# Hybrid attention and convolution layer: far scores over full rows, one head in a bank, parameters transposed later, and a new instruction order

## The chip, the core and the metric

The kernel runs on one core of a Trainium2 chip. The metric is the time of one execution in microseconds (us), taken on the device. PE is TensorE, the matrix engine; DVE is VectorE, ACT is ScalarE, POOL is GpSimd, and SP is the engine that issues most DMAs.

## The reference, cut to what matters

One layer works on x of 1024 tokens by 1024 columns, in fp32. A normed x is projected into seven parts; an attention branch and a convolution branch use them, and one output projection joins both.

```python
h = rmsnorm(x, norm_g)
q, k, v, a_gate, c_val, c_glu, c_gate = split(h @ w_in)   # 1024, 256, 256, 1024, 1024, 1024, 1024 columns
...
for window, dilation in ((128, 1), (512, 4), (2048, 16)):  # 16 query heads, 4 key heads, 64 wide
    o, lse = dilated_window_attention(q, k, v, slopes, window, dilation)
...
y_att = sum(softmax(lses) * outs) * silu(a_gate)
c = layernorm(causal_conv31(c_val * sigmoid(c_glu)) + conv_b) * ln_g + ln_b
y_conv = silu(c) * silu(c_gate)
x = x + concat([y_att, y_conv]) @ w_out
return rmsnorm(x, final_norm_g)
```

## The kernel before, in words

Every fp32 value that TensorE multiplies is split into a high and a low part (names ending in h or hi, l or lo), and a product is the sum of two or three matmuls over these parts. The 5632 columns of the input projection are made 128 at a time: the function `inproj` loads a 128-column block of weights (`raw`), casts it to `wh` and gets `wl` by a DMA that POOL issues, and fills a PSUM bank `ps` with 48 matmuls of 512 columns for the block. What reads a finished bank (`use`) is named in the place that asks for the projection: `project_q` writes the scaled queries of two heads to `qs`, with the high part in the 64 rows of the head's own half and the low part in the other 64 rows (DVE, line 269), and ACT casts them to `qf`, which holds the same queries with the four tokens of a stride apart.

Attention goes by pairs of heads, 0 to 7 (`attend`). Its scores are of two kinds. Near scores, `sc_near`, are those within 128 tokens; far scores, `sc_far`, serve the dilations 4 and 16. A call of `score` makes the scores of both heads for a few units, one PSUM bank `sc` for each head. There are two such banks. `kdh` holds the high part of the keys in both halves of its rows, `kdl` the low part. A near unit is two matmuls over all 128 rows: queries by `kdh` (which is high by high and low by high in one), and queries by `kdl`. The call far0 has 4 units of 96 columns for each head, far1 and far3 have 2 units of 224, and the near calls have 2 units of 256 (one of the first call's is 128). DVE adds a table and takes a minimum from each unit in PSUM (line 284), and ACT takes the exponent; then the bank is free for the next call. The sums over values go to `comb`, which is stored to a tile `y` by SP for one half and added into it by a DMA of POOL (`add_into`, line 298) for the other; then DVE multiplies `y` by the gate `ag` (line 269, 128x1024).

For far scores before the change, the matmuls by `kdl` use only the 64 rows of the head's own half (so low queries by low keys are left out); the two heads' matmuls alternate, one in the upper and one in the lower half of the array, and all of a call form one operation of the plan:

```python
second[j].append((to, q[r], keys(kl)[r], False, last))
...
pl.mm(first + [c for both in zip(*second) for c in both])
```

The convolution is 31 taps on DVE (`convolve`, buffers `c` and `t`, line 269). `parameters` loads the taps, `conv_b`, `ln_g` and `ln_b` as rows and transposes them on PE into the bank `par_ps`.

The order of the work is not written by hand. A class `Plan` records every operation with a modelled cost, and its `order` schedules the list for all engines: a priority from the program position, less a boost of `TUNE`; limits of how many buffers of a group are alive (`LIMITS`); and which projections stand beside which head pair and convolution block (`SECTIONS`). The result is one fixed order for each engine, which the engine follows on the chip and in which it waits where something is late. All matmuls carry line 237 and all transposes line 235.

Of the kernel before, what the change touches and what calls it, by code (L numbers as in the profile page):

```python
# [16 lines left out]
P = 128  # L17
# [6 lines left out]
DH = 64  # L24
# [8 lines left out]


LIMITS = {"x": 5, "raw": 1, "raw_oc": 1, "raw_oa": 2, "wh": 4, "wl": 3, "tab": 1, "e": 7, "pt": 4, "vs": 4, "vc":
          4, "turn": 2, "opsa": 2, "score": 2, "hc": 7, "c": 7, "t": 1, "g": 1, "gl": 7, "y": 2, "ag": 4, "cc": 5,
          "qs": 6, "qf": 4, "kdh": 9, "kdl": 5, "yc": 1, "ya": 2, "zc": 8, "za": 3}

RESERVE = {"e": 7, "pt": 3}
BANKS = {"mm": 3, "sc": 2, "tp": 2, "o": 1}  # L40
WARM = 26
LATE = C_CG + 6 * P
MORE = (8, 8)
TUNE = {"w": 225, "use": 120, "ln": 75, "att": 240, "conv": 15, "wo": 165, "woa": -350, "ap": 50, "wait": 0.2116}
SECTIONS = [("k0 q0 h1 v", 0), ("h2 a0 q1", 1), ("h3 a1 q2", 1), ("a2 q3 h4", 1), ("h5 k1 a3 q4", 1), ("h6 a4 q5",
            1), ("c0 h7 a5 q6", 1), ("a6 c1 a7 q7 c2", 1), ("c5 c4 c3", 1), ("c6 c7", 0)]


def score_tables():
# [112 lines left out]
class Plan:  # L162
    LATENCY = 0.2
    ahead = 267
    near = 574
# [138 lines left out]
    def order(self):  # L304
# [55 lines left out]
        while len(out) < n:  # L360
            best = None
            for e, todo in ready.items():
                now, pick = None, None
                for i in sorted(todo, key=self.prio.__getitem__):
                    t = start_of(i)
                    if t is None:
                        continue
                    soon = t - TUNE["wait"] if self.prio[i] < i - 300 else t
                    if now is None or soon < now - 1e-9:
# [94 lines left out]
def layer_kernel(tc, x, norm_g, w_in, conv_w, conv_b, ln_g, ln_b, w_out, fin_g, tab, out):  # L464
# [3 lines left out]
    def pool(name, space=None):  # L468
# [4 lines left out]
    pl = Plan(tc, {  # L473
        "big": (sb, "big", 4), "c8": (sb, "c8", 1), "c4": (sb, "c4", 33), "c2": (sb, "c2", 5), "st": (sb, "st", 16),
        "sx": (sb, "sx", 6),
        **{k: (ps, k, BANKS[k]) for k in PSUM_KINDS},
    }, LIMITS)
# [35 lines left out]
    def c4(shape, name, dtype=F32):  # L513
        group = name.rstrip("0123456789_")
        return pl.buf("c4", shape, dtype, name, group=group if group in pl.limits else None)

    def bank(kind, name, group=None):
        return pl.buf(kind, [P, 512], F32, name, group=group)
# [24 lines left out]
    hhi = [pl.buf("big", [P, ND, 512], F32R, f"hhi{i}") for i in range(2)]  # L543
# [61 lines left out]
    def parameters():  # L605
        pl.load(rows[0:KT, :], conv_w)
        for j, v in enumerate((conv_b, ln_g, ln_b)):
            pl.load(rows[KT + j:KT + j + 1, :], v.rearrange("(o d) -> o d", o=1))
        b = bank("o", "par_ps")
        pl.mm([(b[:, c * NPAR:(c + 1) * NPAR], rows[0:NPAR, c * P:(c + 1) * P], ident[0:NPAR, 0:NPAR], None, None)  # L610
               for c in range(8)])
        pl.act(par, b[:, 0:8 * NPAR], AF.Copy)
        pl.ts(half_w, par, 0.5, None, ALU.mult)
        for p in range(8):
            g = half_w[:, p * NPAR:p * NPAR + KT + 1].split(2)
            t = taps[:, p * 48:p * 48 + 48].split(3)
            pl.act(t[:, :, 0], g[:, :, 0], AF.Copy)
            pl.act(t[:, 0:15, 1], g[:, 0:15, 1], AF.Copy)
            pl.act(t[:, 0:1, 2], g[:, 0:1, 0], AF.Copy)
            pl.tt(t[:, 1:16, 2], g[:, 1:16, 0], g[:, 0:15, 1], ALU.add)  # L620


    def load_raw(col):
        raw = c4([P, ND, P], f"raw{col}")
        pl.load(raw, w_in[:, col:col + P].rearrange("(c p) n -> p c n", p=P))
        return raw

    def split_w(col, raw, split=split_dma):
        wh, wl = c4([P, ND, P], f"wh{col}", F32R), c4([P, ND, P], f"wl{col}", F32R)
        split(wh, wl, raw)  # L630
        return wh, wl

    def load_w(col):
        if col in ready:
            return ready[col]
        old, pl.boost = pl.boost, TUNE["w"]
        w = split_w(col, load_raw(col), split_r if col >= LATE else split_dma)
# [3 lines left out]
    def inproj(col, use, cuts=((0, 512), (0, 512))):  # L641
        wh, wl = load_w(col)
        for half in range(2):
            b = bank("mm", f"ps{col}_{half}")
            for n0, n1 in zip(cuts[half], cuts[half][1:]):
# [5 lines left out]
                for c in range(0, ND, 2):  # L651
                    pl.mm([(b[:, n0:n1], wl[:, c + i, :], hhi[half][:, c + i, n0:n1], False, c + i == ND - 1)
                           for i in range(2)])
            pl.boost = TUNE["use"]
            use(half, b, slice(half * 512, half * 512 + 512))
# [46 lines left out]
    qs, qf = {}, {}  # L702
# [20 lines left out]
    ag = {}  # L723
# [15 lines left out]
    hc = {}  # L739

    def project_h(p):
        hc[p] = c4([P, 2, 512], f"hc{p}")

        def use_glu(half, b, cs):
            pl.act(hc[p][:, :, half * 256:half * 256 + 256], b.parity(), AF.Tanh, scale=0.5)

        def use_val(half, b, cs):
            h = hc[p][:, :, half * 256:half * 256 + 256]
            pl.stt(h, h, 1.0, b.parity(), ALU.add, ALU.mult)
        cuts = ((0, 512), (0, 512)) if p else ((0, 256, 512), (0, 512))  # L750
        glu, val = inproj(C_GLU + p * P, use_glu, cuts), inproj(C_VAL + p * P, use_val, cuts)
        if p == 0:
            for g in (glu, val, glu, val, glu, val):
                next(g)
                yield 1.0
            for g in (glu, val):
                next(g, None)
        else:
            yield from chain([glu, val])
# [36 lines left out]
    def attend(p):  # L796
# [4 lines left out]
        kh, kl = kd[kv]  # L801
        y = c4([P, 4, 256], f"y{p}")
# [29 lines left out]

        def score(name, units):


            first, second, todo = [], [[], []], []
            for j in range(2):
                sc, o, one = bank("sc", f"sc{p}_{name}_{j}", "score"), 0, []
                for q, keys, t, e, s, near in units[j]:
                    dst = sc[:, o:o + e.cols]  # L840
                    to, r = dst.crossed() if near else dst, slice(j * DH, j * DH + DH)
                    first.append((to, q, keys(kh), not o, False))
                    last = len(todo) % len(units[j]) == len(units[j]) - 1
                    if near:
                        one += [first.pop(), (to, q, keys(kl), False, last)]
                    else:
                        second[j].append((to, q[r], keys(kl)[r], False, last))
                    todo.append((e, dst, t, s))
                    o += e.cols
                if one:  # L850
                    pl.mm(one)
            if first:
                pl.mm(first + [c for both in zip(*second) for c in both])
            for e, dst, t, s in todo:
                pl.add_min(e, dst, t, 3e38, s[:, 0])
                pl.act(e, e, AF.Exp, bias=s[:, 0], scale=-1.0, accum=s[:, 1])

        score("far0", [[far_unit(j, r, 0) for r in range(4)] for j in range(2)])
        yield 3.0
        for r in (0, 2):  # L860
            score(f"far{r + 1}", [[far_unit(j, r, 1), far_unit(j, r + 1, 1)] for j in range(2)])
            yield 2.0
# [4 lines left out]
        for b in (0, 2, 4, 6):  # L867
            score(f"near{b}", [[near_unit(j, b), near_unit(j, b + 1)] for j in range(2)])
            yield 2.0
        w = pl.buf("sx", [P, 4, 2, 2, 4], F32, f"w{p}")  # L870
# [9 lines left out]
        both = f[:, :, 1, :]  # L880
# [19 lines left out]
        for i in range(4):  # L900
# [10 lines left out]
            k0 = 2 * i  # L911
# [3 lines left out]
            o = bank("o", f"on{p}_{i}")  # L915
# [17 lines left out]
        for r0 in (0, 2):  # L933
            whole = turned(f"w{r0}", [(at(2 * r + j), far_e(j, r0 + r, 1)[:, 0:P])
                                      for r in range(2) for j in range(2)], P)
            for r in (r0, r0 + 1):
                part = turned(f"p{r}", [(at(j), far_e(j, r, 0)) for j in range(2)]
                              + [(at(2 + j), far_e(j, r, 1)[:, P:224]) for j in range(2)], 96)
                o = bank("o", f"of{p}_{r}")
                oh = o.split(256)  # L940
                v0, v1 = vc[r][:, 0, kv, :], vc[r][:, 1, kv, :]
                c = (r - r0) * 256
# [6 lines left out]
        if p == NH // 2 - 1:  # L949
            for n in range(2):  # L950
                both = bank("tp", f"y{p}_{n}", "turn")
# [5 lines left out]
        for j in range(2):  # L957
            dst = y[j * DH:(j + 1) * DH]
# [141 lines left out]
    first = project_h(0)  # L1100
    next(first)
    prepare(1)
    parameters()
    make = {"h": project_h, "c": project_cg, "a": project_ag, "q": project_q, "k": project_k}

# [5 lines left out]
    def boosted(name, gen):  # L1111
        while True:
            pl.boost = TUNE[name]
            w = next(gen, None)
            pl.boost = 0
            if w is None:
                return
            yield w

    def section(k, weight, spine, more=()):  # L1120
        nonlocal done
        proj, m = SECTIONS[k]
        hs = [boosted("att", attend(i)) for i in range(done, done + m)]
# [48 lines left out]
```

## Time and profile before

| what | us |
|---|---|
| median of 3 runs | 883.57 |
| lowest and highest | 883.2 and 883.66 |
| the profiled execution | 883.03 |
| its span in the trace | 881.3 |
| PE busy in it | 865.1 (98%) |
| DVE busy | 654.7 (74%) |
| ACT busy | 591.7 (67%) |

The profiled execution lies 1.73 us above its span, and 0.54 us below the median of the runs. An engine's busy time is the time in which the trace shows one of its instructions at work; matmuls overlap their successors, so a row's duration is longer than its distance to the next row, and it is the distance that adds up.

### The profile page before, as it was taken

How to read it: one execution, taken by the hardware profiler on the slowest of the kernel's cores; microseconds unless marked ns; L12 is line 12 of the kernel's file. 1: busy time of each engine (PE TensorE's matmuls, PEld its weight loads, DVE VectorE, ACT ScalarE, POOL GpSimd, SP SyncE). 2: the span in 40 equal slices, each digit the busy share in tenths (PEclk: the TensorE clock that was granted, in tenths of full speed). 3: DMA queues.
4: the chain of work that ended last, by engine and by line, in shares of the span. 5: the costliest groups of instructions: out<-in, count | busy, mean ns of one | idle time of the engine just before them, and what ended most of it. 6: DMA issues, size and time to landing. Idle time of an engine off the chain costs nothing.

```text
span 881.3 us, 12967 instructions
## 1 busy us (share of the span) xinstructions
PE 865.1 (98%) x4458; PEld 722.5 (82%) x4458; DVE 654.7 (74%) x1506; ACT 591.7 (67%) x1392; POOL 53.3 (6%) x69
## 2 busy tenths in 40 slices
PE   8999999999999999999999999999999999999996
PEld 6988888888888888888887888888887778878885
DVE  5659996599699689799789768954559695925333
ACT  5768368767978958958878937885895563714111
POOL 0000001010010010010000110001000000000000
PEclk8899999999999999999999999999999999999999
DMA  8542407354555465445525663545856588787211
GB/s 268 146 95 49 120 3 168 79 117 102 108 103 122 120 123 119 119 73 155 111 57 138 158 143 83 123 120 134 227 190 215 168 299 326 266 263 217 87 48 48
DMA packets 104952, 123.53 MB, mean 140 GB/s; under 512 B 17941, under 2 KB 78357, under 8 KB 104888
## 3 DMA queue, kind: packets, MB, share of 16 engines
q1 hardware_dynamic: 97000, 94.40, 34.6%
q0 software_dynamic: 7888, 28.32, 17.8%
q8 instruction: 35, 0.57, 0.3%
q14 instruction: 29, 0.24, 0.1%
HBM read 65.35 MB, written 24.84 MB: 102 GB/s over the span
## 4 chain that ended last, share of the span: by engine, by line
PE 88%; DMA 4%; DVE 3%; issue 2%; ACT 1%; SPq 0%; POOL 0%; ACTq 0%; POOLq 0%
PE ps L237 51%; PE opsc L237 10%; PE opsa L237 8%; PE sc_near L237 3%; PE on L237 3%; PE sc_far L237 3%; PE of L237 3%; PE tp_p L235 2%; PE tp_m L235 1%; DMA rows<-in_ln_b 1%; PE tp_s L235 1%; DMA yc<-yc_dram 1%; DMA x<-in_x 1%; PE tp_w L235 1%; DMA wl<-raw 1%
## 5 line engine op out<-in xcount | busy, mean ns | idle before, releaser
L237 PE MATMUL ps<-hhi,wh 128*128 128x512 f32 (+1 forms) x720 | 287.6, 400 | 0.0
L237 PE MATMUL ps<-hlo,wh 128*128 128x512 f32 (+1 forms) x720 | 281.4, 392 | 0.4 <-DVE hlo L265 0.4
L237 PE MATMUL ps<-hhi,wl 128*128 128x512 f32 (+1 forms) x720 | 190.0, 396 | 0.1
L237 PEld LDWEIGHTS ps<-hhi,wh 128*128 128x128 f32 x720 | 137.6, 191 | 27.0
L237 PEld LDWEIGHTS ps<-hlo,wh 128*128 128x128 f32 x720 | 137.6, 191 | 26.3 <-DVE hlo L265 0.7
L237 PEld LDWEIGHTS ps<-hhi,wl 128*128 128x128 f32 x720 | 129.6, 190 | 26.6 <-issue 1.0
L252 ACT ACTIVATE e<-e,near 128x256 f32<-128x256 f32 (+1 forms) x256 | 115.1, 489 | 10.3 <-DVE near L265 6.4
L269 DVE SCALAR_TENSOR_TENSOR c<-hc,taps,c 128x511 f32<-128x511 f32 (+14 forms) x120 | 88.5, 738 | 0.2
L269 DVE SCALAR_TENSOR_TENSOR c<-t,taps,c 128x511 f32<-128x511 f32 (+14 forms) x120 | 88.3, 736 | 0.1
L269 DVE SCALAR_TENSOR_TENSOR t<-hc,taps,t 128x511 f32<-128x511 f32 (+6 forms) x112 | 82.4, 736 | 0.1
L237 PE MATMUL opsc<-woc,yhc 128*128 128x512 f32 (+1 forms) x272 | 81.0, 381 | 0.8 <-ACT yhc L250 0.8
L252 ACT ACTIVATE e<-e,far 128x224 f32<-128x224 f32 (+1 forms) x128 | 53.8, 422 | 25.6 <-DVE far L284 20.5
L298 POOL DMA_DIRECT2D wl<-raw x40 | 34.8, 869 | 475.4 <-ACT wl L252 293.1
L237 PEld LDWEIGHTS opsc<-woc,yhc 128*128 128x128 f32 x272 | 50.0, 188 | 11.8 <-ACT yhc L250 1.2
L237 PE MATMUL opsc<-woc,ylc 128*128 128x512 f32 (+1 forms) x136 | 51.8, 381 | 0.5 <-DVE ylc L265 0.5
L252 ACT ACTIVATE fjunk<-zc 128x512 bf16<-128x512 f32 (+1 forms) x17 | 10.3, 606 | 61.6 <-DVE zc L265 61.6
L250 ACT CAST wh<-raw 128x1024 fp32r<-128x1024 f32 x44 | 46.0, 1045 | 1.5 <-DMA raw<-in_w_in 1.5
L284 DVE CUSTOM_DVE_ANT_0 e<-sc_near,tab 128x256 f32<-128x256 f32 (+1 forms) x128 | 44.8, 402 | 2.7 <-PE sc_near L237 2.3
L237 PE MATMUL opsa<-woah,yha 128*128 128x512 f32 x112 | 44.8, 400 | 0.4 <-DVE cc L265 0.3
L252 ACT ACTIVATE e<-e,f 128x224 f32<-128x224 f32 (+1 forms) x128 | 45.2, 438 | 0.0
L237 PE MATMUL opsa<-woah,yla 128*128 128x512 f32 x112 | 44.2, 395 | 0.0
L237 PE MATMUL opsa<-woal,yha 128*128 128x512 f32 x112 | 44.0, 393 | 0.0
(166 smaller groups left out, 1445.1 us busy)
## 6 DMA issues: line engine op xcount, KB each, us to landing
raw<-in_w_in SPq DMA_DIRECT2D x44, 512.0 KB, 5.4
wl<-raw POOLq DMA_DIRECT2D x40, 512.0 KB, 5.1
x<-in_x SPq DMA_DIRECT2D x8, 512.0 KB, 7.1
tab<-in_tab SPq DMA_DIRECT2D x8, 512.0 KB, 4.8
c_dram<-c SPq DMA_DIRECT2D x8, 512.0 KB, 4.4
g_dram<-g SPq DMA_DIRECT2D x8, 512.0 KB, 4.8
raw_oa<-in_w_out SPq DMA_DIRECT2D x8, 512.0 KB, 5.9
cc<-c_dram SPq DMA_DIRECT2D x8, 512.0 KB, 6.6
```

The source lines that it names most:

```text
L235: nc.tensor.transpose(out.ap(), a.ap(), b.ap())
L237: nc.tensor.matmul(out.ap(), a.ap(), b.ap(), start=start, stop=stop)
L250: nc.scalar.copy(out.ap(), x.ap())
L252: nc.scalar.activation(out.ap(), x.ap(), func, **{k: ap_of(v) for k, v in kw.items()})
L269: lambda: self.nc.vector.scalar_tensor_tensor(out.ap(), a.ap(), ap_of(s), b.ap(), op0, op1),
L284: lambda: self.nc.vector.tensor_tensor_reduce(out.ap(), a.ap(), b.ap(), 1.0, ap_of(first), ALU.add, ALU.min, least.ap()),
L298: self.op("POOL", 1.0, lambda: self.nc.gpsimd.dma_start(ap_of(dst), x.ap(), accum_op=ALU.add), [dst], [x, dst])
```

## The change

The far scores are made like the near ones: each unit is queries by `kdh` and then queries by `kdl`, both over all 128 rows, and each head's bank is an operation of its own. The branch that told the two kinds apart goes. Low queries by low keys is now part of the far scores. `pl.hold` makes the transposes of the parameters wait in the plan for the first 128 tokens of `hhi[1]`, the high part of the second half of the normed x. The numbers of the planner change: `use` 120 to 240, `att` 240 to 300, `woa` -350 to -530; the limit of `hc` from 7 to 9 and of `kdl` from 5 to 4; in `SECTIONS`, the projection of v moves from the first section to the second, and c2 from the eighth to the ninth. Of these tables one line stands here:

```diff
-TUNE = {"w": 225, "use": 120, "ln": 75, "att": 240, "conv": 15, "wo": 165, "woa": -350, "ap": 50, "wait": 0.2116}
+TUNE = {"w": 225, "use": 240, "ln": 75, "att": 300, "conv": 15, "wo": 165, "woa": -530, "ap": 50, "wait": 0.2116}
...
         b = bank("o", "par_ps")
+        pl.hold = [hhi[1][:, 0:4, 0:P]]
         pl.mm([(b[:, c * NPAR:(c + 1) * NPAR], rows[0:NPAR, c * P:(c + 1) * P], ident[0:NPAR, 0:NPAR], None, None)
...
-            first, second, todo = [], [[], []], []
+            todo = []
             for j in range(2):
                 sc, o, one = bank("sc", f"sc{p}_{name}_{j}", "score"), 0, []
                 for q, keys, t, e, s, near in units[j]:
                     dst = sc[:, o:o + e.cols]
-                    to, r = dst.crossed() if near else dst, slice(j * DH, j * DH + DH)
-                    first.append((to, q, keys(kh), not o, False))
+                    to = dst.crossed() if near else dst
                     last = len(todo) % len(units[j]) == len(units[j]) - 1
-                    if near:
-                        one += [first.pop(), (to, q, keys(kl), False, last)]
-                    else:
-                        second[j].append((to, q[r], keys(kl)[r], False, last))
+                    one += [(to, q, keys(kh), not o, False), (to, q, keys(kl), False, last)]
                     todo.append((e, dst, t, s))
                     o += e.cols
-                if one:
-                    pl.mm(one)
-            if first:
-                pl.mm(first + [c for both in zip(*second) for c in both])
+                pl.mm(one)
```

The order that follows changes in many places. Three of them are shown.

On PE near the start, before (xT are transposes of x, ps2560 is the first bank of the projection whose weight columns begin at 2560):

```order
L237 MATMUL ps3584_0_222<-hhi0_197,wl3584_233 128x256 x8
L235 MATMUL xT02_0_266<-ident_66,x2_137 128x128 x4
L235 MATMUL xT02_1_273<-ident_66,x2_137 128x128 x4
L235 MATMUL par_ps_284<-ident_66,rows_151 128x34 x8
L235 MATMUL xT03_0_295<-ident_66,x3_139 128x128 x4
L237 MATMUL ps2560_0_301<-hhi0_197,wh2560_282 128x256
```

At the same place of the same engine after the change:

```order
L235 MATMUL xT02_0_266<-ident_66,x2_137 128x128 x4
L235 MATMUL xT02_1_273<-ident_66,x2_137 128x128 x4
L235 MATMUL xT03_0_285<-ident_66,x3_139 128x128 x4
L237 MATMUL ps2560_0_292<-hhi0_197,wh2560_282 128x256
L237 MATMUL ps2560_0_292<-hlo0_206,wh2560_282 128x256
```

The transposes into `par_ps` no longer stand between those of x; they come later, between projection matmuls and xT11_0.

On PE in head pair 5, the near scores before (sc5_near2_0 is the bank of the call near2 for the first head of the pair, near2_1 for the second; a line of dots stands for the rest of a bank's four matmuls):

```order
L237 MATMUL sc5_near2_0_4783<-kdh2_3565,qs10_4529 128x4x2x32
L237 MATMUL sc5_near2_0_4783<-kdl2_3597,qs10_4529 128x4x2x32
...
L237 MATMUL sc5_near2_1_4791<-kdh2_3565,qs11_4538 128x4x2x32
...
L237 MATMUL sc5_near4_0_4800<-kdh2_3565,qs10_4529 128x4x2x32
...
L237 MATMUL sc5_near4_1_4811<-kdh2_3565,qs11_4538 128x4x2x32
```

The same calls after the change (ps4608_1 is a bank of a projection):

```order
L237 MATMUL sc5_near2_0_4792<-kdh2_3590,qs10_4597 128x4x2x32
...
L237 MATMUL ps4608_1_4715<-hhi1_397,wl4608_4515 128x512 x2
L237 MATMUL sc5_near2_1_4805<-kdh2_3590,qs11_4602 128x4x2x32
...
L237 MATMUL ps4608_1_4715<-hhi1_397,wl4608_4515 128x512 x4
L237 MATMUL sc5_near4_0_4821<-kdh2_3590,qs10_4597 128x4x2x32
...
L237 MATMUL sc5_near4_1_4829<-kdh2_3590,qs11_4602 128x4x2x32
```

Before, the near calls of this pair follow each other, 28 matmuls from near0_0 to near6_0 without a projection matmul between; now two or four projection matmuls stand between most of them, 16 in all from near0_0 to near6_0, and the product of `y4` by its gate, which stood on DVE between the units of near0_0 and near0_1, stands ahead of far1.

On DVE ahead of head pair 6, before (c7 and t7 are the convolution's block 7, qs12 and qs13 the queries of pair 6 from the bank ps768_0, y5 the product by the gate for pair 5):

```order
L269 SCALAR_TENSOR_TENSOR c7_5192<-t7_5197,taps_77,c7_5192 128x509
L269 SCALAR_TENSOR_TENSOR qs12_5360<-ps768_0_5321,qs12_5360 64x512
L269 SCALAR_TENSOR_TENSOR qs13_5366<-ps768_0_5321,qs13_5366 64x512
L269 SCALAR_TENSOR_TENSOR c7_5192<-hc7_4958,taps_77,c7_5192 128x508
L269 SCALAR_TENSOR_TENSOR t7_5197<-hc7_4958,taps_77,t7_5197 128x508
L269 SCALAR_TENSOR_TENSOR y5_5302<-y5_5302,ag5_5280 128x1024
```

And after the change:

```order
L269 SCALAR_TENSOR_TENSOR c7_5193<-t7_5191,taps_77,c7_5193 128x510
L269 SCALAR_TENSOR_TENSOR c7_5193<-hc7_4928,taps_77,c7_5193 128x509
L269 SCALAR_TENSOR_TENSOR y5_5297<-y5_5297,ag5_5276 128x1024
L269 SCALAR_TENSOR_TENSOR qs12_5357<-ps768_0_5320,qs12_5357 64x512
L269 SCALAR_TENSOR_TENSOR qs13_5362<-ps768_0_5320,qs13_5362 64x512
L269 SCALAR_TENSOR_TENSOR t7_5191<-hc7_4928,taps_77,t7_5191 128x509
```

`y5` has moved from behind qs12 and qs13 to ahead of them.

## Rows read from the trace of the kernel before

**Rows 1.** The page: the span, and each engine's busy time.

```profile
span 881.3 us, 12967 instructions
...
PE 865.1 (98%) x4458; PEld 722.5 (82%) x4458; DVE 654.7 (74%) x1506; ACT 591.7 (67%) x1392; POOL 53.3 (6%) x69
```

**Rows 2.** Windows: us, busy by engine, PE's granted clock, DMA share, GB/s.

```profile
45.00:464.50 419.50, 419.37 (x2235) 352.32 (x2233) 359.12 (x866) 322.50 (x807) 34.91 (x41) 1.00 0.46 103
464.50:472.70 8.20, 6.38 (x31) 5.23 (x32) 8.12 (x35) 7.35 (x29) 0.91 (x1) 0.79 0.67 160
```

**Rows 3.** Timeline of PE: start, duration, what, [idle before].

```profile
22.88 1.04 PE L235 MATMUL par_ps<-ident,rows 34*128 34x34 f32 x8 [3.15 <-DMA rows<-in_ln_b]
...
24.61 0.56 PE L237 MATMUL ps<-hhi,wh 128*128 128x256 f32 x1
```

**Rows 4.** Timeline of ACT at the same place.

```profile
22.46 1.05 ACT L250 CAST wh<-raw 128x1024 fp32r<-128x1024 f32 x1 [0.98 <-DMA raw<-in_w_in]
```

**Rows 5.** Timeline of PE: a far0 and a far1 call of pair 1.

```profile
183.89 0.99 PE L237 MATMUL sc_far<-kdh,qf 128*128 128x96 f32 x8
184.80 0.65 PE L237 MATMUL sc_far<-kdl,qf 64*128 64x96 f32 x8
185.38 0.76 PE L237 MATMUL ps<-hhi,wl 128*128 128x512 f32 x2
185.98 0.39 PE L237 MATMUL ps<-hhi,wh 128*128 128x512 f32 x1
...
193.91 0.60 PE L237 MATMUL sc_far<-kdh,qf 128*128 128x224 f32 x4
...
194.84 0.50 PE L237 MATMUL ps<-hhi,wh 128*128 128x512 f32 x1
195.18 0.39 PE L237 MATMUL ps<-hlo,wh 128*128 128x512 f32 x1
195.41 0.40 PE L237 MATMUL ps<-hhi,wh 128*128 128x512 f32 x1
```

**Rows 6.** Timeline of PE: the near calls of pair 5.

```profile
464.76 0.40 PE L237 MATMUL ps<-hlo,wh 128*128 128x512 f32 x1
...
467.22 0.36 PE L237 MATMUL sc_near<-kdh,qs 128*128 128x256 f32 x1 [0.58 <-DVE near L284]
467.42 0.28 PE L237 MATMUL sc_near<-kdl,qs 128*128 128x256 f32 x1
467.54 0.28 PE L237 MATMUL sc_near<-kdh,qs 128*128 128x256 f32 x1
...
468.91 0.41 PE L237 MATMUL sc_near<-kdh,qs 128*128 128x256 f32 x1 [0.97 <-DVE near L284]
469.12 0.41 PE L237 MATMUL sc_near<-kdl,qs 128*128 128x256 f32 x1
...
472.65 0.63 PE L237 MATMUL ps<-hhi,wl 128*128 128x512 f32 x2
```

**Rows 7.** Timeline of DVE at the same place.

```profile
466.99 1.22 DVE L269 SCALAR_TENSOR_TENSOR y<-y,ag 128x1024 f32<-128x1024 f32 x1
468.13 0.28 DVE L284 CUSTOM_DVE_ANT_0 e<-sc_near,tab 128x128 f32<-128x128 f32 x1
```

**Rows 8.** POOL, tile y, 522 to 533 us: issues, time to landing.

```profile
L298 POOL DMA_DIRECT2D y<-comb x2: 822/822/823, 522.1 to 523.0; - x2
...
DMA to landing us min/median/max: 8.1/8.3/8.4
```

**Rows 9.** The page: all weight loads by POOL's queue, us to landing at the end.

```profile
wl<-raw POOLq DMA_DIRECT2D x40, 512.0 KB, 5.1
```

**Rows 10.** Timelines of DVE, ACT and PE ahead of pair 6's far0.

```profile
529.48 1.41 DVE L269 SCALAR_TENSOR_TENSOR qs<-ps,qs 64x512 fp32r<-64x512 f32 x2 [1.43 <-ACT qs L252]
...
530.20 2.14 ACT L250 CAST qf<-qs 128x512 fp32r<-128x512 f32 x2 [0.75 <-DVE qs L269]
...
532.66 0.99 PE L237 MATMUL sc_far<-kdh,qf 128*128 128x96 f32 x8
```

More of the change, by code (lines that the diff above doesn't have):

```diff
@@ L35 @@
 LIMITS = {"x": 5, "raw": 1, "raw_oc": 1, "raw_oa": 2, "wh": 4, "wl": 3, "tab": 1, "e": 7, "pt": 4, "vs": 4, "vc":
-          4, "turn": 2, "opsa": 2, "score": 2, "hc": 7, "c": 7, "t": 1, "g": 1, "gl": 7, "y": 2, "ag": 4, "cc": 5,
-          "qs": 6, "qf": 4, "kdh": 9, "kdl": 5, "yc": 1, "ya": 2, "zc": 8, "za": 3}
+          4, "turn": 2, "opsa": 2, "score": 2, "hc": 9, "c": 7, "t": 1, "g": 1, "gl": 7, "y": 2, "ag": 4, "cc": 5,
+          "qs": 6, "qf": 4, "kdh": 9, "kdl": 4, "yc": 1, "ya": 2, "zc": 8, "za": 3}
 RESERVE = {"e": 7, "pt": 3}
@@ L43 @@
 MORE = (8, 8)
-TUNE = {"w": 225, "use": 120, "ln": 75, "att": 240, "conv": 15, "wo": 165, "woa": -350, "ap": 50, "wait": 0.2116}
-SECTIONS = [("k0 q0 h1 v", 0), ("h2 a0 q1", 1), ("h3 a1 q2", 1), ("a2 q3 h4", 1), ("h5 k1 a3 q4", 1), ("h6 a4 q5",
-            1), ("c0 h7 a5 q6", 1), ("a6 c1 a7 q7 c2", 1), ("c5 c4 c3", 1), ("c6 c7", 0)]
+TUNE = {"w": 225, "use": 240, "ln": 75, "att": 300, "conv": 15, "wo": 165, "woa": -530, "ap": 50, "wait": 0.2116}
+SECTIONS = [("k0 q0 h1", 0), ("v a0 q1 h2", 1), ("h3 a1 q2", 1), ("a2 q3 h4", 1), ("h5 k1 a3 q4", 1), ("h6 a4 q5",
+            1), ("c0 h7 a5 q6", 1), ("a6 c1 a7 q7", 1), ("c2 c5 c4 c3", 1), ("c6 c7", 0)]
 def score_tables():
```

## The prediction

> **What bounds the kernel now.** I read the page first. The span is 881.3 us and PE is busy in 865.1 of it, 98%; DVE is busy for 654.7 and ACT for 591.7 [rows 1]. So the end is set by PE's own work and by the few places where PE has none. The windows say where these are: from 45 to 464.5 us PE is busy for 419.37 of 419.50 us at a granted clock of 1.00, and between 464.5 and 472.7 us it is busy for 6.38 of 8.20 at a mean clock of 0.79 [rows 2]. The rest of the idle time is in the first 45 us and at the end. A change can therefore do three things here: make a group of PE's instructions cheaper or dearer, take away one of those holes, or open a new one. DVE, ACT, POOL and the DMAs matter only where PE comes to wait for them.
>
> I then read PE's timeline at four places: the hole at the start, one far0 and one far1 call, the hole in head pair 5, and the place ahead of pair 6 where the new order puts something else in front of what PE needs. The distance from one row's start to the next is the price of a row; durations overlap.
>
> **The far scores.** A full-row far matmul costs 0.114 us: eight take from 183.89 to 184.80 [rows 5]. The eight 64-row matmuls behind them take from 184.80 to 185.38, 0.58, and the two projection matmuls after that take 0.60 where two cost 0.46 (0.23 each, from 195.18 to 195.41), so 0.14 is lost at the way back [rows 5]. A far0 call costs 1.49 + 0.14 = 1.63. A far1 or far3 call takes 0.93 from 193.91 to 194.84, and the next projection matmul costs 0.34 for 0.23: 1.04 in all [rows 5]. There are 8 calls of far0 (16 matmuls each) and 16 of far1 and far3 (8 each). With full rows I take 0.114 for every matmul, no loss at the edges. Far0 becomes 16 x 0.114 = 1.82, +0.19 each, +1.5 for eight; far1 and far3 become 0.91, -0.13 each, -2.1 for sixteen. Together **-0.6**. No row shows a far unit of 224 columns with full rows by `kdl`. Bounds: at 0.105 for these (a 512-column matmul takes 0.23, so 224 columns alone would take 0.10) the sixteen give -3.2 and the sum -1.7; at the 0.12 of a near matmul with 256 columns [rows 6] for all, far0 gives +2.3, the others -1.3, and the sum is +1.0. The 96-column row is the nearest for one and the near row for the other, both full-row pairs of the same two operands, so the value lies between.
>
> The change puts twice the rows to work for the 128 matmuls by `kdl`. What the row shows against the halves being worth it is the 0.073 for each 64-row matmul where two at a time would make 0.057, and the 0.11 to 0.14 lost behind each call. The Trainium skill speaks against the change here: TensorEngine Tiling (Array Packing), Overview, Theoretical Speedup, gives up to 2x where the contraction is 64 or less. By that figure alone, 128 matmuls that stood in 64 slots would cost 64 x 0.114 = 7.3 us more as an estimate. The same page says under Tiling Modes, Key Properties, that a change of mode drains the engine, and the lost time at the edges in this trace agrees.
>
> **The hole in pair 5.** From 464.76 to 472.65 PE has one projection matmul and the 28 near matmuls from near0_0 to near6_0 with no projection work between [rows 6]. At full clock these take 0.23 + 28 x 0.12 = 3.6 us; they take 7.89, so the hole costs 4.3. PE waits 0.58 and 0.97 for DVE to empty a score bank; from 468.91 the rows are 0.21 apart instead of 0.12, the lower level of the clock (1.2 GHz instead of 2.4), and the last 16 take 3.74 instead of 1.9 [rows 6]. The cause is on DVE: the 128x1024 product of `y4` takes from 466.99 to 468.13 just between two banks [rows 7]. In the new order that product stands ahead of far1, and 16 projection matmuls (3.7 us) stand among the same 28, which makes 7.1 us of PE work for which DVE needs about as long. I take the whole **-4.3**. It could be less if the wait only moves; the bound is a wait of both sizes again, 1.6, taken below.
>
> **The start.** The transposes into `par_ps` wait 3.15 us for the row of ln_b, to 22.88 [rows 3]. With them gone from this place, PE goes on to xT03_0 and to the projection at 2560. That one needs `wh2560`, whose cast ends at 23.51, after a wait of 0.98 for its own raw weights [rows 4]. So the projection begins at 23.5 instead of 24.61 [rows 3]: -1.1, and the 1.04 of the parameters' transposes is paid later, between two groups that PE has ready. Sum **-0.1**; from -1.1 (they fall into a later wait of the first 45 us) to 0.
>
> **A new wait ahead of pair 6.** The new DVE order puts `y5` ahead of qs12 and qs13, behind which stand `qf` on ACT and then far0 of pair 6 on PE. `y5` needs two adds that POOL issues at 522.1 and 523.0 and that land 8.1 to 8.4 us later [rows 8], so at 531.4. It did not matter before, since qs12 began at 529.48 ahead of it [rows 10]. Now: y5 from 531.4 to 532.6 (1.22, as in [rows 7]), one qs 0.70 to 533.3, one qf 1.07 to 534.4 [rows 10]. PE was at far0 at 532.66 and has two projection matmuls fewer ahead of it in the new order, so it wants it at 532.2. It waits **+2.0** (0 if the adds land sooner; 2.3 with the slower landing). DVE holds the convolution's steps behind `y5`, which nothing on PE needs there.
>
> **Small waits.** Several pairs now have near calls with little between, and DVE and PE need about the same time for them. I take **+0.4**, from 0 to 1.6 (the two waits of pair 5 once more). The other numbers of the planner move work that lies beside saturated PE, and I cost it at nothing: PE has its 0.13 us of idle time in 419.5 [rows 2], and what covers the rest is the projection matmuls. If that cover fails in a pair, it costs what it cost in pair 5.
>
> **The sum**, against the profiled execution's 883.03 (span 881.3 and 1.73 around it; 0.54 under the median of the runs): 883.03 - 0.6 - 4.3 - 0.1 + 2.0 + 0.4 = **880.4**.
>
> **The rivals.**
> 1. The adds of `y` land as most DMAs of that queue do: the weight loads land 5.1 us after issue [rows 9]. Then y5 is ready at 528.1, done at 529.3, and qs12 is not later than before. No wait: 880.4 - 2.0 - 0.4 = 878. For it: the place in the queue and the load on it depend on the new order. Against it: the only rows for these two adds say 8.1 to 8.4.
> 2. The wait moves instead of going. A wait of 2 us ahead of pair 6 is longer than the 0.58 and 0.97 after which the clock fell in pair 5; if the clock falls again over as many matmuls, 1.8 us come on top, 882.2; with the small waits at their upper end 883.4. Nothing has changed then that can be measured.
> 3. Slower: the time lost around a far call does not come from the 64 rows but from the change of banks and operands, and stays. Without it, far0 is 12 slots of 0.114, 1.37, so 0.26 is lost at its edges, and far1 is 6 slots, 0.68, with 0.36 lost. With full rows and the same losses they cost 2.08 and 1.27: 8 x 0.45 + 16 x 0.23 = +7.3 instead of -0.6, and the time is 888.3. It makes the kernel slower by more than 0.2% once the far term passes +4.3. Against it: the near rows, full-row pairs in their own banks, stand 0.12 apart with no loss [rows 6]. It comes to the same number as the rule of the array packing page of the Trainium skill, quoted above.
> 4. The start's gain is kept whole and the far term is at its lower end: 883.03 - 4.3 - 1.7 - 1.1 = 875.9 without the wait at pair 6.
>
> **How the numbers follow.** The sum as it stands has 0.45, rival 1 has 0.25, rival 2 has 0.22, rival 3 has 0.05, rival 4 has 0.03. What a measurement of this kernel can tell from no change is about 0.2%, 1.8 us: 881.8 to 885.3 is the same. The sum's own spread leaves 0.03 of it above 881.8, and rival 2 is above that bound in 0.16 and below it in 0.06. Faster: 0.42 + 0.25 + 0.06 + 0.03 = 0.76. Same: 0.03 + 0.16 = 0.19. Slower: 0.05. The range goes from the foot of rival 4, 876.0, to the upper end of rival 2, 883.3, with rival 3 and a little else outside.
>
> **What would show it.** In the trace after: far calls of 1.82 and 0.91 with the next projection matmul at 0.23; no window in pair 5 with a clock under 1.00; the first projection at 2560 at 23.5 and the parameters' transposes later without a wait; a wait of PE of about 2 us at pair 6's far0, with DVE waiting for a DMA into `y` ahead of it. The prediction is wrong if far calls keep 0.3 us at their edges, if PE waits for score banks in other pairs for more than some 2 us in all, or if the clock falls at pair 6. A time under 877 would mean a gain at a place that I have not priced.

## The result and the profile after

The changed kernel takes 877.04 us (median of 4 runs, 876.23 to 877.6); the kernel before takes 883.38 (4 runs, 881.77 to 883.66). The ratio is 0.9932, with a 95% interval of 0.9919 to 0.9946: faster by about 6 us. I had forecast 880.4, in a range of 876.0 to 883.3. The direction and the largest term, the hole in pair 5, held. The loss that the sum added ahead of pair 6 did not come, so the time is that of the first rival (878), and the gain is more than twice the one I summed up. The profiled execution after the change took 877.6, against 883.03 before; PE's granted clock had the same mean, 0.85, over the first 45 us of both.

The page and the windows of the changed kernel (columns as in [rows 2]) answer to [rows 1, 2]:

```profile
span 875.8 us, 12969 instructions
...
PE 861.9 (98%) x4458; PEld 724.2 (83%) x4458; DVE 653.2 (75%) x1506; ACT 590.4 (67%) x1392; POOL 53.3 (6%) x69
```

```profile
464.50:472.70 8.20, 8.20 (x52) 7.32 (x52) 8.20 (x36) 8.02 (x28) 0.89 (x1) 1.00 0.47 105
...
45.00:640.00 595.00, 595.00 (x3202) 505.51 (x3201) 488.92 (x1217) 471.26 (x1192) 51.24 (x60) 1.00 0.50 114
```

PE works through the whole stretch from 45 to 640 us at full clock: the hole of pair 5 is gone, and no other came. PE's timeline of the changed kernel has the start, a call of far1 or far3 in pair 2, the near calls of pair 5 from their first matmul to the row behind near6_0, and the second head's far0 in pair 6, which answer to [rows 3, 5, 6]:

```profile
22.11 1.07 PE L235 MATMUL xT<-ident,x 128*128 128x128 f32 x4 [2.17 <-DVE hlo L265]
23.91 0.58 PE L237 MATMUL ps<-hhi,wh 128*128 128x256 f32 x1 [0.73 <-ACT wh L250]
...
257.93 0.26 PE L237 MATMUL sc_far<-kdh,qf 128*128 128x224 f32 x1
...
258.82 0.40 PE L237 MATMUL ps<-hhi,wh 128*128 128x512 f32 x1
259.05 0.39 PE L237 MATMUL ps<-hlo,wh 128*128 128x512 f32 x1
...
464.25 0.23 PE L237 MATMUL sc_near<-kdh,qs 128*128 128x128 f32 x1
...
471.27 0.39 PE L237 MATMUL ps<-hhi,wh 128*128 128x512 f32 x1
...
528.51 0.21 PE L237 MATMUL sc_far<-kdh,qf 128*128 128x96 f32 x1
...
529.34 0.69 PE L237 MATMUL ps<-hhi,wl 128*128 128x512 f32 x2
529.87 0.40 PE L237 MATMUL ps<-hhi,wh 128*128 128x512 f32 x1
```

A call with 224 columns takes 0.89, and the next projection matmul 0.23: 0.15 less than the 1.04 of before. One head's far0 takes 0.83, and the two projection matmuls behind it 0.53 for 0.46: 0.90, so 1.80 for a call, 0.17 more than the 1.63 of before. 16 x 0.15 - 8 x 0.17 = 1.0 us gained. In pair 5 the 28 near matmuls and the 16 projection matmuls that now stand among them take 7.02 us, from 464.25 to 471.27; at 0.23 for each of the 16 that leaves 3.3 for the 28, which took 7.66 in [rows 6] (7.89 with one projection matmul). So the hole's 4.3 us are gained back, and 883.03 - 4.3 - 1.0 = 877.7, where the profiled execution took 877.6. That leaves 0.1 us for all the rest, the start and the end included.

### The profile page after: what moved, and what is told of

It reads as the page before. It is cut to its first block, busy times and chain, and to the rows that moved or that the text cites. A ratio compares the mean times of both kernels' runs of the same rounds, so it can differ in the third digit from the quotient of the medians.

```text
span 875.8 us, 12969 instructions
## 1 busy us (share of the span) xinstructions
PE 861.9 (98%) x4458; PEld 724.2 (83%) x4458; DVE 653.2 (75%) x1506; ACT 590.4 (67%) x1392; POOL 53.3 (6%) x69
## 4 chain that ended last, share of the span: by engine, by line
PE 95%; DMA 2%; DVE 1%; issue 0%; ACT 0%; SPq 0%; DVEq 0%; ACTq 0%
PE ps L237 56%; PE opsc L237 10%; PE opsa L237 9%; PE sc_near L237 3%; PE on L237 3%; PE sc_far L237 3%; PE of L237 3%; PE tp_p L235 2%; PE tp_m L235 2%; DMA raw<-in_w_in 2%; PE tp_s L235 1%; DMA x<-in_x 1%; PE tp_w L235 1%; PE xT L235 1%; DVE cc L265 1%; PE y L237 0%
## 5 line engine op out<-in xcount | busy, mean ns | idle before, releaser
L252 ACT ACTIVATE e<-e,f 128x96 f32<-128x96 f32 (+1 forms) x128 | 45.3, 438 | 0.0
```

The source lines that it names most:

```text
L252: nc.scalar.activation(out.ap(), x.ap(), func, **{k: ap_of(v) for k, v in kw.items()})
```

## The experiments

Ratios are to the kernel before, run on the same chip each time, with their 95% intervals. Orders were kept instruction by instruction except where "computed anew" is said.

**The far scores alone, in the old order.** Low queries by low keys join the far scores.

```diff
-                        second[j].append((to, q[r], keys(kl)[r], False, last))
+                        second[j].append((to, q, keys(kl), False, last))
```

> The kernel before, every engine's order kept instruction by instruction; only the far matmuls by kdl use 128 rows instead of 64 (so low queries by low keys join the far scores). Theory (the loss around a far call comes from the 64 rows): the 128 far matmuls by kdl and by kdh cost 0.112 each, far0 goes from 1.63 to 1.8 and far1 and far3 from 1.04 to 0.89, so 8 x 0.17 - 16 x 0.15 = -1.1 us, about 882.3 on the scale of 883.4 for the kernel before (ratio 0.9987); the hole in pair 5 stays. Rival (the halves are worth two at a time, or the loss belongs to the banks): +7.3 us, 890.7 (ratio 1.008).

Measured: 882.43 us, ratio 0.9992 (0.9983 to 1.0002). The time alone does not tell it from no change, but it excludes +7.3. PE's timeline of this kernel has the price:

```profile
184.03 0.99 PE L237 MATMUL sc_far<-kdh,qf 128*128 128x96 f32 x8
184.85 1.05 PE L237 MATMUL sc_far<-kdl,qf 128*128 128x96 f32 x8
185.75 0.69 PE L237 MATMUL ps<-hhi,wl 128*128 128x512 f32 x2
186.27 0.40 PE L237 MATMUL ps<-hhi,wh 128*128 128x512 f32 x1
...
194.21 0.60 PE L237 MATMUL sc_far<-kdh,qf 128*128 128x224 f32 x4
...
195.09 0.40 PE L237 MATMUL ps<-hhi,wh 128*128 128x512 f32 x1
195.33 0.40 PE L237 MATMUL ps<-hlo,wh 128*128 128x512 f32 x1
```

Far0 is 1.72 + 0.06 = 1.78 and far1 0.88, with 0.24 behind it: 8 x 0.15 - 16 x 0.15 = -1.2 us against [rows 5]. The third rival of the prediction, that the loss belongs to the banks and operands, falls.

**The halves one head at a time, in the new order.** Low queries by low keys are left out again.

```diff
-                    one += [(to, q, keys(kh), not o, False), (to, q, keys(kl), False, last)]
+                    one.append((to, q, keys(kh), not o, False))
...
+                        low.append((to, q[r], keys(kl)[r], False, last))
...
-                pl.mm(one)
+                pl.mm(one + low)
```

> The changed kernel in its own order, except that the far matmuls by kdl use 64 rows, each head by itself behind its matmuls by kdh (no two heads side by side; low queries by low keys left out again). Theory (the loss comes with each change from 128 rows to 64 and back, about 0.09 each way and 0.1 for the next projection matmul): 64 such stretches at some 0.2 to 0.3 us, 8 to 12 us slower overall if each 64-row matmul still takes about 0.11: 886 to 890. Rival (the loss needs two heads side by side or two banks): 877.

Measured: 893.71 us, ratio 1.0112 (1.0097 to 1.0127), some 16 us above the changed kernel. PE's timeline, two banks of a call with 224 columns and one of far0:

```profile
189.62 0.37 PE L237 MATMUL sc_far<-kdh,qf 128*128 128x224 f32 x2
189.92 0.48 PE L237 MATMUL sc_far<-kdl,qf 64*128 64x224 f32 x2
190.33 0.48 PE L237 MATMUL sc_far<-kdh,qf 128*128 128x224 f32 x2
190.75 0.48 PE L237 MATMUL sc_far<-kdl,qf 64*128 64x224 f32 x2
191.15 0.50 PE L237 MATMUL ps<-hhi,wh 128*128 128x512 f32 x1
191.49 0.40 PE L237 MATMUL ps<-hlo,wh 128*128 128x512 f32 x1
...
253.72 0.64 PE L237 MATMUL sc_far<-kdl,qf 64*128 64x96 f32 x4
254.30 0.96 PE L237 MATMUL ps<-hhi,wl 128*128 128x512 f32 x3
```

Each 224-column matmul that stands next to a change between 128 and 64 rows takes about 0.2 instead of 0.11, the full-row pair from 190.33 to 190.75 too. So the loss does come with the changes, and it is dearer than I had: 1.53 + 0.11 instead of 0.89, 0.37 for each of two stretches. A stretch of four halves of 96 columns costs 0.26 (1.05 and 0.11 behind it instead of 0.90). There are 48 stretches, not the 64 that I had counted: 16 x 0.26 + 32 x 0.37 = 16.0 us, the whole of it. Four halves alone of 96 columns take 0.58, as long as eight side by side in [rows 5]. Side by side, then, a second half costs nothing. The Trainium skill, TensorEngine Tiling (Array Packing), Overview, Theoretical Speedup, gives up to 2x for it, and the trace agrees at 96 columns; at 224 the changes eat it.

**y4 out of the way of pair 5, in the old order.**

```diff
-L269 SCALAR_TENSOR_TENSOR y_4693<-y_4693,ag_4332 128x1024
 L284 ISA e_10_4779,near_4772<-sc_near_1_4765,tab_4267 128x128
```

The row stands again behind the last unit of near6 on DVE, and the store of y4 behind one weight load on SP.

> The kernel before in its own order, except that y4's product by the gate stands behind the last near unit of pair 5 on DVE (and its store to y_dram behind one weight load on SP). The 28 near matmuls still stand without projection work between. Theory A, as the prediction has it (the product between two banks causes the hole): the waits shrink to under 0.6, the clock does not fall, -3 to -4 us: 879.8 on the scale of 883.4 (ratio 0.996). Theory B (the near calls without projection work between are the cause, since DVE needs 0.35 for each unit and 0.7 for each convolution step): the 0.97 wait shrinks, other waits of some 0.9 and 0.25 come up in the same calls, at most -1.3 us: 882 to 883.4.

Measured: 882.50 us, ratio 0.9987 (0.9978 to 0.9996). PE's timeline in the same calls, and the window:

```profile
463.91 0.40 PE L237 MATMUL ps<-hlo,wh 128*128 128x512 f32 x1
...
466.37 0.36 PE L237 MATMUL sc_near<-kdh,qs 128*128 128x256 f32 x1 [0.58 <-DVE near L284]
...
468.04 0.36 PE L237 MATMUL sc_near<-kdh,qs 128*128 128x256 f32 x1 [0.40 <-DVE near L284]
...
469.38 0.36 PE L237 MATMUL sc_near<-kdh,qs 128*128 128x256 f32 x1 [0.63 <-DVE near L284]
...
470.62 2.01 PE L237 MATMUL ps<-hhi,wl 128*128 128x512 f32 x8
```

```profile
464.00:473.00 9.00, 7.25 (x43) 5.80 (x42) 8.66 (x41) 8.90 (x35) 0.92 (x1) 1.00 0.58 123
```

The clock stays at its higher level, but three waits of 1.6 us in all remain. From 463.91 to 470.62 it takes 6.71 us where [rows 6] have 7.89: 1.2 of the 4.3 us was y4's place, the fall of the clock included. The other 3.1 stay with the 28 near matmuls that have no projection work between: DVE, which empties their banks, is busy for 8.66 of the 9.00 us. Theory B holds, though its waits have other sizes than I gave them.

**The term of +2.0 by itself: y5 first, in the old order.**

```diff
+L269 SCALAR_TENSOR_TENSOR y_5302<-y_5302,ag_5280 128x1024
 L269 SCALAR_TENSOR_TENSOR qs_5360<-ps_0_5321,qs_5360 64x512
...
-L269 SCALAR_TENSOR_TENSOR y_5302<-y_5302,ag_5280 128x1024
```

> The kernel before in its own order, except that y5's product by the gate stands ahead of qs12 and qs13 on DVE, as in the new order; its weight load raw4736 runs beside the adds. This is the prediction's term of +2.0 by itself. Theory: y5 starts at 531.4, qs12 ends at 533.3, qf12 at 534.4, PE waits 1.7 us ahead of far0 at 532.66: 885.1 where the kernel before has 883.4 (ratio 1.002), 886.9 if the clock falls. Rival (the adds' landing is set by something else, or PE's queue hides it): 883.4.

Measured: 887.79 us, ratio 1.0045 (1.0028 to 1.0062). PE's timeline ahead of far0 of pair 6, and the window around it:

```profile
535.95 0.65 PE L237 MATMUL sc_far<-kdh,qf 128*128 128x96 f32 x4 [1.72 <-ACT qf L250]
536.98 1.09 PE L237 MATMUL sc_far<-kdh,qf 128*128 128x96 f32 x4 [0.39 <-ACT qf L250]
```

```profile
530.00:545.00 15.00, 12.89 (x52) 10.24 (x51) 7.70 (x18) 7.76 (x13) 0.00 (x0) 0.77 0.34 88
```

The wait of 1.72 is as worked out; the second one, 0.39 for the second head's queries, was not in it. The clock falls behind them (0.77 in this window's mean): about 4 us in all, where I had 3.5 with a fall of the clock. The runs spread from 885.56 to 890.39, and the profiled one, 889.89, is near the upper end.

**The weight load back beside the adds, in the new order.** One row of SP's order moves.

```diff
 L301 DMA y_5297<-comb_5020 64x1024 x2
+L295 DMA raw_5386<-in_w_in 128x8x128
 L301 DMA y_dram<-y_5297 128x1024
-L295 DMA raw_5387<-in_w_in 128x8x128
```

> The changed kernel in its own order, except that SP issues the weight load raw4736 ahead of the store of y5 to y_dram, as the kernel before does, and not behind it. Theory (the adds into y5 land late when that load runs beside them): they land 8 us after issue instead of 5.2 to 6.1, at about 525.9; y5, which stands ahead of qs12, ends at 527.1, qf12 at 528.9, and PE, which wants far0 of pair 6 at 527.1, waits about 1.8 us: 878.9 where the changed kernel has 877.0, up to 880.7 if PE's clock falls. Rival (the landing doesn't depend on that load): 877.0, no wait.

Measured: 881.08 us, ratio 0.9970 (0.9959 to 0.9981), some 3.4 us above the changed kernel by the ratios and 4.0 by the medians. The adds of POOL into y in this kernel:

```profile
DMA to landing us min/median/max: 7.6/7.8/7.9
```

The timelines of DVE and PE there, and the window in which the clock is down:

```profile
525.79 1.23 DVE L269 SCALAR_TENSOR_TENSOR y<-y,ag 128x1024 f32<-128x1024 f32 x1 [2.43 <-DMA y<-comb]
...
528.92 0.31 PE L237 MATMUL sc_far<-kdh,qf 128*128 128x96 f32 x1 [1.39 <-ACT qf L250]
...
530.88 0.40 PE L237 MATMUL sc_far<-kdl,qf 128*128 128x96 f32 x1
531.08 0.41 PE L237 MATMUL sc_far<-kdh,qf 128*128 128x96 f32 x1
```

```profile
528.90:534.50 5.60, 5.58 (x26) 4.87 (x27) 4.88 (x13) 3.19 (x8) 0.00 (x0) 0.70 0.44 121
```

The same of the changed kernel, with SP's queue, shows the difference:

```profile
DMA to landing us min/median/max: 5.2/5.7/6.1
```

```profile
523.92 1.22 DVE L269 SCALAR_TENSOR_TENSOR y<-y,ag 128x1024 f32<-128x1024 f32 x1 [0.90 <-DMA y<-comb]
...
525.17 0.34 SPq L301 DMA_DIRECT2D y_dram<-y  x1
525.61 1.47 SPq L295 DMA_DIRECT2D raw<-in_w_in  x2
```

In the changed kernel SP issues that load only behind the store of y5, which itself waits for the adds. In the kernel before it went out at 519.74, ahead of the adds (SP's queue in its trace):

```profile
519.74 0.57 SPq L295 DMA_DIRECT2D raw<-in_w_in  x1
```

With the load beside them the adds take 7.8 us, without it 5.7. Some 2 us after the wait of 1.39 the clock falls: rows of 96 columns are 0.2 apart, the lower of the two levels, until about 534 (the window's mean is 0.70). The nine matmuls from 530.88 to 534.20 take 3.3 us where the same nine take 1.8 in the changed kernel, from 529.00 to 530.80. So the clock costs 1.5 us, as much again as the wait.

**Far scores new, numbers old, order computed anew; and the numbers with the later transposes, far scores old.** Both are parts of the change's own diff. The first has low queries by low keys, the second leaves them out as before.

> The kernel before with the far scores as in the changed kernel, the planner's numbers and the parameters' transposes as before, order computed anew. In its order 16 projection matmuls stand among the near calls of pair 5, as in the changed kernel. Theory (splitting the far operation in two alone changes the order enough, the numbers carry nothing): hole gone, -4.3, far -1.1: 878.0 on the scale of 883.4 (ratio 0.994). Rival (the new numbers are what takes the waits away): the hole or other score waits remain, 881 to 882.5 (ratio 0.997 to 0.999).

> The kernel before with the planner's new numbers and the later transposes of the parameters, far scores as before in 64 rows, order computed anew. In its order projection matmuls stand between the near calls of pair 5 too. Theory (the hole is an accident of the old order and any new order loses it): -4.3 with nothing from the far scores, 879.1 on the scale of 883.4 (ratio 0.995). Rival (the hole belongs to the far scores' joint operation for both heads): the hole stays, 883 (ratio 0.999 to 1.001).

Measured: 882.18 us, ratio 0.9986 (0.9976 to 0.9996), for the far scores with the old numbers, and 878.40, ratio 0.9947 (0.9933 to 0.9960), for the numbers with the later transposes. A window of each, the far scores first:

```profile
45.00:640.00 595.00, 595.00 (x3193) 506.06 (x3192) 487.97 (x1212) 462.64 (x1170) 51.24 (x60) 1.00 0.50 114
```

```profile
45.00:640.00 595.00, 593.77 (x3182) 499.75 (x3181) 488.12 (x1211) 466.09 (x1179) 51.23 (x60) 1.00 0.50 112
```

Neither has the hole: the first waits nowhere in this stretch, the second twice for far units, 1.2 us in all. So the hole was an accident of one order, and the rival that ties it to the joint operation falls. But the first loses about as much at another place. PE's waits in that kernel (total, times, longest):

```profile
PE rb L237 <- DVE lst L269: 3.1, 1, 3.1
...
PE opsa L237 <- DVE yla L265: 1.7, 1, 1.7
```

In its order only 10 projection matmuls stand between head pair 7 and the layer norm, and the norm's rb stands ahead of the output projection, where it waits for DVE. The old sections alone do not decide that: the kernel before has them too, with 2 such matmuls, and its rb stands behind 48 matmuls of the output projection. My theory that the numbers carry nothing fell.

**Far scores and the sections alone, order computed anew.**

```diff
-SECTIONS = [("k0 q0 h1 v", 0), ("h2 a0 q1", 1), ("h3 a1 q2", 1), ("a2 q3 h4", 1), ("h5 k1 a3 q4", 1), ("h6 a4 q5",
+SECTIONS = [("k0 q0 h1", 0), ("v a0 q1 h2", 1), ("h3 a1 q2", 1), ("a2 q3 h4", 1), ("h5 k1 a3 q4", 1), ("h6 a4 q5",
```

> The kernel before with the far scores as in the changed kernel and the new list of sections (v in the second, c2 in the ninth); the boosts, the limits and the parameters' transposes as before; order computed anew. In its order 50 projection matmuls stand between the last scores' sums and the layer norm's mean, as in the changed kernel, where far scores with the old sections have 10. Theory (of the planner's numbers the sections alone matter, by what stands ahead of the output projection): 877.5 on the scale of 883.4 for the kernel before (ratio 0.9933). Rival (the boosts and limits matter too): 879 to 882.

Measured: 880.56 us, ratio 0.9974 (0.9965 to 0.9983). The wait for rb is gone, but in pair 2 there is one that the changed kernel hasn't. DVE and PE there:

```profile
254.62 1.22 DVE L269 SCALAR_TENSOR_TENSOR y<-y,ag 128x1024 f32<-128x1024 f32 x1 [1.91 <-DMA y<-comb]
...
258.62 0.34 PE L237 MATMUL sc_far<-kdh,qf 128*128 128x224 f32 x1 [1.62 <-DVE far L284]
```

```profile
258.60:270.00 11.40, 11.38 (x69) 10.08 (x70) 11.40 (x49) 10.53 (x41) 0.90 (x1) 1.00 0.45 99
```

It is the mechanism that I had feared in pair 6: the product of y waits for its adds, and far units that PE needs stand behind it. Here the clock stays at its higher level behind a wait of 1.62, as the window shows. The rival holds, in that the sections alone are not enough: the boosts, the limits or the later transposes matter too, by which of these collisions an order has. Which one of them avoids this wait I did not try, and the wait is about half of the 3.7 us by which this kernel is above the changed one; where the rest lies is not shown.

**Far0 in halves again, the rest in full rows.** Low queries by low keys are left out of far0. First with only its matmuls moved within the new order, then with the order computed anew (the lines are those of the second):

```diff
+                    if halves:
+                        low[j].append((to, q[r], keys(kl)[r], False, last))
...
+            if halves:
+                pl.mm(first + [c for both in zip(*low) for c in both])
```

> The changed kernel in its own order, except that far0 alone is made as before: the matmuls by kdl in 64 rows, the two heads side by side, issued where head 1's matmuls stood (head 0's move there). Theory (64-row pairs take 0.11 a pair at 96 columns, where they save, and 0.2 at 224, where they don't): far0 goes from 1.79 to 1.63, 8 x 0.16 = -1.3 us against the changed kernel, 875.7 where that has 877.0 (ratio to the kernel before 0.9915). Rival (full rows are better at both widths, or the wait for the second head's queries eats it): 877 to 878 (ratio 0.993 to 0.994).

> The changed kernel with far0 alone as before (one operation for both heads, kdl in 64 rows side by side), far1 and far3 in full rows, and the order computed anew, so that the joint operation finds its place. Theory: far0 costs 1.63 for 1.79, 8 x 0.16 = -1.3 us: 875.7 where the changed kernel has 877.0 (ratio to the kernel before 0.9915). Rival (the joint operation brings waits for the second head's queries and banks again, as in the kernel with only its matmuls moved): 877 or above.

Measured: 877.27 us, ratio 0.9933 (0.9917 to 0.9950), with its matmuls only moved, and 874.89, ratio 0.9909 (0.9896 to 0.9922), with the order anew. In the first the rival holds: PE waits twice for far units on DVE, probably since head 0's bank is filled later:

```profile
PE sc_far L237 <- DVE far L284: 0.5, 2, 0.3
```

In the second a far0 call (pair 2, PE's timeline) is back at 1.50 with 0.57 for the next two projection matmuls, and no such wait is listed:

```profile
247.10 0.99 PE L237 MATMUL sc_far<-kdh,qf 128*128 128x96 f32 x8
...
248.60 0.73 PE L237 MATMUL ps<-hhi,wl 128*128 128x512 f32 x2
249.17 0.39 PE L237 MATMUL ps<-hhi,wh 128*128 128x512 f32 x1
```

I ran it and the changed kernel once more on one chip:

> The changed kernel itself, on the same chip as the next one: 877.0, ratio to the kernel before 0.993.

> The changed kernel with far0 alone as before and the order computed anew, once more, beside the changed kernel on one chip. Theory (1.3 us from far0 and fewer small losses): 874.9, some 2 us under the changed kernel. Rival (the earlier 874.9 was a chip's difference): within 0.1% of it.

Measured: 877.70 us, ratio 0.9933 (0.9921 to 0.9946), for the changed kernel, and 876.14, ratio 0.9916 (0.9903 to 0.9930), for the version with far0 in halves. It had the lower median both times, by 2.1 us across chips and by 1.6 on one, where its far0 alone gives 8 x 0.17 = 1.4; the intervals of the two still overlap, so the size is not settled.

## Why the prediction was right or wrong

- **The hole in pair 5**: right in place and size. 8.20 of 8.20 us are busy at a clock of 1.00, and 4.3 us of the gain are there. The cause that I named first was only a part: with y4's product away the same 28 matmuls still lose 3.1 us. What counted more was the projection matmuls among them, which I had listed second; 7.1 us were worked out for the stretch with them, and it takes 7.02. No run has them there with y4 left in its old place, so their share is inferred: what y4's place leaves.
- **The far scores**: -0.6 forecast, -1.0 by the rows after, -1.2 by those of the kernel with this change alone. The 224-column matmuls take 0.11 and not 0.114; 0.07 is lost behind each head's far0, which I had left out. The term was of the right sign and inside its bounds.
- **The start**: -0.1 forecast. The 3.15 us wait became 2.17 ahead of xT03_0 for the split of x, which I had not named, and 0.73 for the cast of the weights, which I had. The projection starts at 23.91 instead of 24.61, 0.4 later than the 23.5 of the forecast, and the parameters' transposes cost 0.6 later, so the term comes to the forecast's size. The clock over the first 45 us differs from one execution of the same kernel to the next (0.85 and 0.96 in two of the changed kernel's), which moves the time by more than this term.
- **The new wait ahead of pair 6**: this step failed. I took 8.1 to 8.4 us for the adds' landing from a trace in which a weight load ran beside them, and did not look at what the new order of SP does with that load. It puts it behind the store of y5. The adds land in 5.2 to 6.1, y5 costs DVE 0.90 of waiting, and PE never waits: the first rival, for a reason that I could have read. The mechanism itself is sound: with the load put back the wait is 1.39, and it comes with a fall of the clock, so the term would have been 3.4 to 4.0 and not 2. The second rival had priced that at 3.8. The sum also slipped: far0 wanted at 532.2 and qf ready at 534.4 make 2.2, not 2.0.
- **The small waits**: +0.4 forecast, nothing measured; PE is busy for 595.00 of 595.00 us from 45 to 640.
- **The planner's numbers at nothing**: wrong as a general statement. With the new far scores and the old numbers the kernel takes 882.18; the numbers, with the later transposes, are worth 5 us beside the far scores and nearly as much without them. Beside the far scores it is by the waits for rb and the output projection, which the sum had nowhere; without them it is mostly the hole, which the sum had priced. The boosts, the limits and the transposes were never run each by itself.

So the forecast of 880.4 missed the profiled execution's 877.6 by the two losses that it added, 2.0 and 0.4, and by 0.4 of the far scores: 2.8, which is the whole of it. That the measured time still lies in the range is owed to the rivals without the wait ahead of pair 6 (1 and 4), which set its lower part; I had given them 0.28 together.

## What to carry to other kernels

When a scheduler is run anew, most of the gain or loss can come from which collisions its order happens to have, and not from the part that was changed; split the two by keeping the order and changing the part, and the other way round. Before a landing time from the old trace is used in a new order, look at which other transfers the new order lets run beside it: follow every queue, SP's too. Where PE is the bound, a wait of some 1.5 us can cost twice itself or more when the clock falls behind it (1.39 us cost 3.4 to 4.0), but it need not: behind one of 1.62 us the clock stayed up.

## What the hardware showed that I had not expected

- Next to a change between 128 and 64 rows every 224-column matmul takes 0.2 us instead of 0.11, on both sides of the change; at 96 columns the four halves take 0.58 in all, alone or two side by side. Halves therefore pay in a call with eight of 96 columns and not in one with four of 224. Whether a 64-row matmul of 224 columns away from such a change would take 0.11 is not shown, since none stood there.
- One weight load of 512 KB beside two adding DMAs of 256 KB lengthens their landing from 5.7 to 7.8 us (pair 6 of the changed kernel, with nothing else moved).
- PE's clock fell to its lower level some 2 us after a wait of 1.39 us, for about 3 us. It did not fall after three waits of 0.40 to 0.63 within 4 us, nor after one of 1.62 us in the kernel with the far scores and the sections alone. What makes the difference is not shown.
